# A causal convolution's last tiles: taps divided anew between four engines, and silus interleaved with products

## The chip, the cores and the metric

The kernel runs on one core of a Trainium2 chip. The metric is the device time of one execution in microseconds. Smaller is better. The engines are named as in the profile: PE is TensorE's matmul, PEld its weight load, DVE is VectorE, ACT is ScalarE, POOL is GpSimd and SP issues most DMAs.

## The reference

The program is a two-layer trunk of a streaming encoder, in float32, for 256 positions of 1024 channels. Each layer computes half a feed-forward block, a mixer, and half a feed-forward block, each on a normalized input and added to `h`. The mixer of the first layer is a convolution module, and the change is in it; that of the second is an attention.

```python
def conv_module(h, w_pw1, w_dw, g_norm, w_pw2):
    u = h @ w_pw1
    a, b = jnp.split(u, 2, axis=-1)
    u = a * jax.nn.sigmoid(b)
    u = lax.conv_general_dilated(          # causal, depthwise, width 31
        u, w_dw[:, None, :].astype(u.dtype), window_strides=(1,),
        padding=[(CONV_WIDTH - 1, 0)],
        dimension_numbers=("NWC", "WIO", "NWC"),
        feature_group_count=D_MODEL)
    u = jax.nn.silu(rmsnorm(u, g_norm))
    return u @ w_pw2
```

So each of 1024 channels is a sum over 31 taps, each a product of a shifted row with one weight per channel. The norm is over all channels of one position, so every channel has to be there before the first silu.

## The kernel before

**Layout.** Channels lie on the 128 partitions, in eight tiles (`k` from 0 to 7), and the 256 positions along the free axis, in two halves of 128, the first rows (`tb` = 0) and the second rows (`tb` = 1). `V` holds the gated input with 30 columns of zeros ahead of it, so that tap `j` of a tile is `V[:, k, j + start : j + stop]` times the column `dw[:, k, j]`.

**Who computes taps.** Three lists divide the 31 taps of each tile. An entry is (tile, first tap, end of taps, half), and half 2 means all 256 columns at once.

- `CONV_DVE`, in `taps_dve`: VectorE multiplies and accumulates in one instruction per tap, into two accumulators by turns (lines 777 and 779). Line 785 adds the two at the end.
- `CONV_POOL`, in `taps_pool`: per tap ScalarE makes a product (line 805, tile `prod`, six buffers) and GpSimd adds it (line 806), into two accumulators by turns. Line 816 adds the two. The first two taps are copies of ScalarE (line 801).
- `CONV_PE`, in `taps_pe`: TensorE multiplies with a diagonal matrix of the tap's weights (line 826). The diagonals are made long before, by ScalarE, beside the first feed-forward block. The taps of tiles 6 and 7 of one half share one PSUM bank `y`.

Tiles 6 and 7 (`CONV_LAST`) come last and are shared: in the first rows, tile 6 has 19 taps on ScalarE and GpSimd and 12 on TensorE, and tile 7 has 13 on VectorE and 18 on TensorE. In the second rows it is 19 and 12, and 24 and 7. The other tiles are each of one engine alone.

**The end of the convolution**, for each half, in `ends`:

1. Line 922: VectorE adds the parts of tile 6, then of tile 7 (`Y`).
2. Line 838: ScalarE squares each tile (`sq`). Line 844: TensorE adds the squares over the channels (`ms`), tile by tile in the order of `CONV_ORDER`; tiles 6 and 7 are last.
3. In `normed`: VectorE takes the mean (line 860, `msc`), GpSimd raises it to the power -1/2 (line 862, `rc`), ScalarE makes a diagonal of it (line 864, `dg`), TensorE spreads it over the partitions (line 866, `rb`).
4. For each tile: VectorE multiplies (line 871, `z`) and ScalarE takes the silu (line 873, `Z`). Tiles 4 to 7 come first (`rows_order`) and are used as they are. For tiles 0 to 3 the silu is also taken rounded (line 875, `Zh`), and VectorE makes the rest (line 876, `Zl`, "low").
5. The products with `cw2` into `o`: two plain matmuls for each of tiles 4 to 7 (line 954), then two times three split ones for each of tiles 0 to 3 (`mm3`, lines 280, 283 and 284). In the loop, `n` or `f` counts the tiles in the order of `rows_order`.

**What sets the order.** The framework's scheduler puts each engine's instructions in a fixed order, by dependencies, by priority (functions marked `urgent` go ahead), and by a timing of its own. `order(a, b)` is an edge that says only that `a` comes after `b`. The kernel uses it to place the totals and `rb` among TensorE's taps: `done[1]` is the list of TensorE's second-row taps, of which five stand ahead of the last total of the first rows, nine between it and `rb`, and five after `rb`. In `taps_dve`, `after` places four of VectorE's second-row taps ahead of the mean, five between the mean and the eight `z`, and the others behind. In `taps_pool`, the products of the second rows' tile 6 from the tenth tap on come after `dg`, and their adds after the power. In the products with `cw2`, the total of the second rows comes after the pair n = 4, `rb` after the pair n = 6, and the first column half of n = 7 after `rb`.

`load_ahead` starts the loads and casts of the next block's weights. A cast stands behind the latest urgent instructions of its engine.

Of the kernel before, what the change touches and what calls it, by code (L numbers as in the profile page):

```python
# [46 lines left out]

CONV_DVE = ((0, 0, 31, 0), (0, 0, 31, 1), (2, 0, 31, 2), (4, 0, 31, 2), (5, 0, 31, 2), (7, 0, 13, 0), (7, 0, 24, 1))  # L50
CONV_POOL = ((1, 0, 31, 0), (1, 0, 31, 1), (3, 0, 31, 2), (6, 0, 19, 0), (6, 0, 19, 1))
CONV_PE = ((6, 19, 31, 0), (7, 13, 31, 0), (6, 19, 31, 1), (7, 24, 31, 1))

CONV_MID = {3: 10, 5: 29}
CONV_FIRST = (0, 1)
CONV_LAST = (6, 7)

# [26 lines left out]
def trunk(ctx: ExitStack, tc: tile.TileContext, x, xt, pos, invf, gains, gfin, wdw,  # L84
# [21 lines left out]
    def bank(tag, name):  # L106
        return ps.tile([P, 512], F32, tag=tag, name=uid(name), bufs=BANKS[tag])
# [185 lines left out]
    def tbs(tb):  # L293
        return slice(tb * P, (tb + 1) * P)
# [423 lines left out]
    def conv_in(act, X, make_next):  # L718
# [46 lines left out]
        odd = {}  # L765
        slot = [0]

        def taps_dve(k, j0, j1, t, after={}):

            slot[0] ^= 1  # L770
            c = slice(slot[0] * S, slot[0] * S + t.stop - t.start)
            out = Y[:, k, t]
            for j in range(j0, j1):
                v, w = V[:, k, j + t.start:j + t.stop], dw[:, k, j:j + 1]
                y = acc[(j - j0) % 2][:, c]
                if j - j0 < 2:
                    ins = nc.vector.tensor_scalar(y, v, w, None, op0=ALU.mult)
                else:
                    ins = nc.vector.scalar_tensor_tensor(out if j == j1 - 1 else y, v, w, y, op0=ALU.mult, op1=ALU.add)  # L779
# [5 lines left out]
            nc.vector.tensor_add(out, acc[(j1 - j0) % 2][:, c], out)  # L785

        last_prod = [None]
        last_sum = [None]

        def taps_pool(k, j0, j1, t, after={}):  # L790

            if j1 - j0 < TAPS and k not in part:
                part[k] = act.tile([P, S], F32, name=uid("part"))
            if k not in odd:
                odd[k] = act.tile([P, S], F32, tag=f"odd{k % 2}", name=uid("odd"))
            y = [(part[k] if k in part else Y[:, k, :])[:, t], odd[k][:, t]]
            for j in range(j0, j1):
                v, w = V[:, k, j + t.start:j + t.stop], dw[:, k, j:j + 1]
                o = y[(j - j0) % 2]
                if j - j0 < 2:  # L800
                    nc.scalar.activation(o, v, AF.Copy, scale=w)
                else:
                    p = act.tile([P, S], F32, tag="prod", name=uid("prod"), bufs=6)
                    p = p[:, :t.stop - t.start]
                    prod = nc.scalar.activation(p, v, AF.Copy, scale=w)
                    ins = nc.gpsimd.tensor_tensor(o, o, p, op=ALU.add)
                    if last_prod[0] is not None:
                        order(prod, last_prod[0].ins)
                        order(ins, last_sum[0].ins)
                    if "power" in after and j >= j0 + 10:  # L810
                        order(prod, after["diagonal"].ins)
                        order(ins, after["power"].ins)
                    last_prod[0], last_sum[0] = prod, ins
                    if (k, j - j0, t.start) == (CONV_LAST[0], 7, 0):
                        nc_silu.append(prod)
            last_sum[0] = nc.gpsimd.tensor_tensor(y[0], y[0], y[1], op=ALU.add)
# [18 lines left out]
        def square(k, t):  # L835
            if k not in sq:
                sq[k] = act.tile([P, S], F32, tag="sq", name=uid("sq"), bufs=4)
            return nc.scalar.activation(sq[k][:, t], Y[:, k, t], AF.Square)
# [17 lines left out]
        @urgent  # L856
        def normed(tb, after=()):

            ms = small.tile([P, 1], F32, tag="msc", name=uid("msc"))
            mean = nc.vector.tensor_scalar(ms, msb[tb][:, :1], 1.0 / D, EPS, op0=ALU.mult, op1=ALU.add)  # L860
            rc = small.tile([P, 1], F32, tag="rc", name=uid("rc"))
            power = nc.gpsimd.tensor_tensor(rc, ms, neghalf, op=ALU.pow)
            dg = act.tile([P, P], F32, tag="dg", name=uid("dg"), bufs=2)
            diagonal = nc.scalar.activation(dg, ident, AF.Copy, scale=rc)
            rb = bank("AC"[tb], "rb")
            brow[tb] = nc.tensor.matmul(rb[:, :P], ones, dg, start=True, stop=True)
            for a in after:
                order(brow[tb], a.ins)
            for k in rows_order:
                z = act.tile([P, P], F32, tag="z", name=uid("z"), bufs=6)  # L870
                zi = nc.vector.tensor_mul(z, Y[:, k, tbs(tb)], rb[:, :P])
                g = G[:, g0 + k:g0 + k + 1]
                nc.scalar.activation(Z[:, k, tbs(tb)], z, AF.Silu, scale=g)
                if k < KT - CONV_PLAIN:
                    nc.scalar.activation(Zh[:, k, tbs(tb)], z, AF.Silu, scale=g)
                    nc.vector.tensor_sub(Zl[:, k, tbs(tb)], Z[:, k, tbs(tb)], Zh[:, k, tbs(tb)].bitcast(F32))
            return mean, power, diagonal, zi

        halves = (tbs(0), tbs(1), every)
        for items, f in ((CONV_DVE, taps_dve), (CONV_POOL, taps_pool)):  # L880
# [34 lines left out]
        def ends(tb, after, after_row):  # L915

            t = tbs(tb)

            @urgent
            def add():  # L920
                for k in CONV_LAST:
                    a = nc.vector.tensor_add(Y[:, k, t], y[tb][k], part[k][:, t] if k in part else Y[:, k, t])
# [8 lines left out]
            mean, power, diagonal, z = normed(tb, (after_row,))  # L931
            steps_of.update({0: a, 4: mean, 9: z, "power": power, "diagonal": diagonal})
# [12 lines left out]
        def mm(n, tb, d):  # L945
            f = rows_order[n]
            after = ()
            if (tb, d) == (0, 0):
                after = [brow[1]] if n == KT - 1 else ()
            w = loaded[conv_block[-1 - f // 2]]  # L950
            c = slice(f % 2 * D + d * 512, f % 2 * D + d * 512 + 512)
            start, stop = n == 0, n == KT - 1
            if f >= KT - CONV_PLAIN:
                return nc.tensor.matmul(o[tb, d], Z[:, f, tbs(tb)], w[:, c], start=start, stop=stop)  # L954
# [398 lines left out]
```

## Time and profile before

| what | value |
|---|---|
| median of 3 runs | 927.15 us (927.1 to 928.87) |
| the profiled execution | 927.98 us |
| its span, first to last instruction | 926.2 us |
| mean granted TensorE clock | 0.999 |
| TensorE busy | 912.5 us, 99% of the span |
| VectorE, ScalarE, GpSimd busy | 682.2, 537.2 and 224.9 us |
| taps on TensorE, tiles 6 and 7 | from 247.23 us on |
| first product with `cw2`, first rows | 261.27 us |
| first product with `cw2`, second rows | 275.04 us |

In the timeline a row gives start, length, engine, source line and operation, then the written tile, the read ones, the shapes and how many instructions are merged in the row. In brackets at its end stands how long the engine had been idle and which instruction ended that. The profile's span leaves out 1.78 us of the execution's time, which lie around it.

### The profile page before, as it was taken

What the parts mean: (1) busy time and instruction counts of PE and PEld (TensorE: products, weight loads), DVE (VectorE), ACT (ScalarE), POOL (GpSimd) and SP (SyncE); (2) the same over time, 40 slices, a digit from 0 to 9 for tenths busy, and PEclk for the clock granted to TensorE, in tenths of its full rate; (3) what the DMA queues carried; (4) which work ended last, traced back from release to release, by engine and by line L of the source; (5) the groups of instructions that cost most, each with busy time, mean ns of one, the idle gap of its engine ahead of it and who ended that gap; (6) DMA issues with size and microseconds to landing.
All of it is one profiled execution on the core that took longest, in us unless ns stands there. A gap on an engine that the chain in (4) does not pass through costs nothing.

```text
span 926.2 us, 12404 instructions
## 1 busy us (share of the span) xinstructions
PE 912.5 (99%) x4315; PEld 757.9 (82%) x4315; DVE 682.2 (74%) x1050; ACT 537.2 (58%) x932; POOL 224.9 (24%) x329
## 2 busy tenths in 40 slices
PE   8999999999999999999999999999999999999997
PEld 6888887898967888888888888888898778888886
DVE  5776877789967667787976667978666476667875
ACT  6955555669847545455574445555667374544653
POOL 0101232379921110232210003223200011003223
PEclk9999999999999999999999999999999999999999
DMA  9986556653306867566756675656441556774751
GB/s 331 346 278 232 186 191 213 251 182 138 138 1 245 297 231 233 182 193 225 281 219 235 228 245 176 200 213 246 182 183 46 182 206 243 251 246 135 227 192 46
DMA packets 60399, 191.58 MB, mean 207 GB/s; under 512 B 11184, under 2 KB 33328, under 8 KB 40752
## 3 DMA queue, kind: packets, MB, share of 16 engines
q1 hardware_dynamic: 59760, 190.09, 59.0%
q8 instruction: 34, 0.56, 0.2%
q10 hardware_dynamic: 576, 0.69, 0.2%
q14 instruction: 29, 0.24, 0.1%
HBM read 178.17 MB, written 12.58 MB: 206 GB/s over the span
## 4 chain that ended last, share of the span: by engine, by line
PE 85%; DVE 5%; ACT 3%; DMA 3%; issue 2%; POOL 1%; SPq 0%; POOLq 0%; ACTq 0%; DVEq 0%
PE u L284 16%; PE u L280 16%; PE u L283 16%; PE o L280 5%; PE o L283 5%; PE o L284 5%; DVE lo L171 3%; PE gate L734 3%; PE u L734 3%; DMA raw<-in_f1w 2%; PE o L954 2%; PE p L280 1%; PE p L283 1%; PE p L284 1%; ACT hi L167 1%
## 5 line engine op out<-in xcount | busy, mean ns | idle before, releaser
L171 DVE TENSOR_TENSOR lo<-raw,hi 128x1024 fp32r<-128x1024 f32 (+1 forms) x246 | 297.7, 1247 | 70.4 <-ACT hi L167 70.0
L167 ACT CAST hi<-raw 128x1024 fp32r<-128x1024 f32 (+1 forms) x250 | 248.0, 1046 | 143.7 <-PE u L284 108.4
L284 PE MATMUL u<-hi,Xl 128*128 128x512 f32 x688 | 267.8, 390 | 0.7 <-DVE Xl L341 0.7
L280 PE MATMUL u<-lo,Xh 128*128 128x512 f32 x688 | 268.1, 390 | 0.0
L283 PE MATMUL u<-hi,Xh 128*128 128x512 f32 x688 | 267.7, 389 | 0.0
L284 PEld LDWEIGHTS u<-hi,Xl 128*128 128x128 f32 x688 | 129.1, 188 | 28.4 <-DVE Xl L341 1.6
L280 PEld LDWEIGHTS u<-lo,Xh 128*128 128x128 f32 x688 | 129.1, 188 | 27.2 <-DVE lo L171 0.5
L283 PEld LDWEIGHTS u<-hi,Xh 128*128 128x128 f32 x688 | 129.1, 188 | 26.6
L181 POOL TENSOR_TENSOR sums<-raw 128x1024 f32<-128x1024 f32 x20 | 54.0, 2698 | 160.2 <-DMA raw<-in_f2w 51.4
L280 PE MATMUL o<-lo,Gh 128*128 128x512 f32 (+1 forms) x236 | 91.4, 387 | 0.7 <-DVE lo L171 0.7
L283 PE MATMUL o<-hi,Gh 128*128 128x512 f32 (+1 forms) x236 | 91.0, 386 | 0.0
L284 PE MATMUL o<-hi,Gl 128*128 128x512 f32 (+1 forms) x236 | 91.0, 386 | 0.0
L628 POOL TENSOR_TENSOR sx<-gb 128x128 f32<-128x128 f32 x20 | 10.4, 520 | 314.8 <-DMA gb<-gd 314.8
L620 ACT CAST Gh<-gb 128x512 fp32r<-128x512 f32 (+2 forms) x48 | 25.6, 539 | 68.0 <-DMA gb<-gd 67.8
L621 DVE TENSOR_TENSOR Gl<-gb,Gh 128x512 fp32r<-128x512 f32 (+2 forms) x48 | 33.2, 707 | 36.5 <-ACT Gh L620 36.5
L779 DVE SCALAR_TENSOR_TENSOR acc<-V,dw,acc 128x128 f32<-128x128 f32 (+1 forms) x171 | 57.5, 416 | 0.0
L189 ACT CAST hi<-sums 128x1024 fp32r<-128x1024 f32 x40 | 40.9, 1052 | 26.7 <-PE u L284 13.8
L190 DVE TENSOR_TENSOR lo<-sums,hi 128x1024 fp32r<-128x1024 f32 x40 | 56.1, 1435 | 0.0
L280 PEld LDWEIGHTS o<-lo,Gh 128*128 128x128 f32 x236 | 44.3, 188 | 10.8 <-DVE lo L171 2.0
L284 PEld LDWEIGHTS o<-hi,Gl 128*128 128x128 f32 x236 | 44.3, 188 | 9.0
L283 PEld LDWEIGHTS o<-hi,Gh 128*128 128x128 f32 x236 | 44.3, 188 | 8.8
L189 ACT CAST hi<-raw 128x512 fp32r<-128x512 f32 (+1 forms) x40 | 31.4, 833 | 28.2 <-PE o L284 23.3
(247 smaller groups left out, 1344.6 us busy)
## 6 DMA issues: line engine op xcount, KB each, us to landing
raw<-in_f2w SPq DMA_DIRECT2D x66, 1024.0 KB, 4.8
raw<-in_f1w SPq DMA_DIRECT2D x64, 1024.0 KB, 5.0
raw<-in_cw SPq DMA_DIRECT2D x12, 1024.0 KB, 5.1
gd<-gt SPq DMA_DIRECT2D x160, 64.0 KB, 2.7
gb<-gd SPq DMA_DIRECT2D x40, 256.0 KB, 2.9
raw<-in_wo SPq DMA_DIRECT2D x4, 1024.0 KB, 4.9
raw<-in_wuq SPq DMA_DIRECT2D x3, 1024.0 KB, 4.8
raw<-in_f1w SPq DMA_DIRECT2D x8, 256.0 KB, 6.5
```

Of the source, the lines that this page charges most:

```text
L167: behind(nc.scalar.copy(hi[:, c], raw[:, c]))
L171: behind(nc.vector.tensor_sub(lo[:, c], raw[:, c], hi[:, c].bitcast(F32)))
L181: behind(nc.gpsimd.tensor_tensor(t[:, 0:2, :], v[:, 0:4:3, :], v[:, 1:2, :].to_broadcast([P, 2, 512]), op=ALU.add))
L189: behind(nc.scalar.copy(hi[:, c0:c1], x[:, c0:c1]))
L190: behind(nc.vector.tensor_sub(lo[:, c0:c1], x[:, c0:c1], hi[:, c0:c1].bitcast(F32)))
L280: mm = nc.tensor.matmul(o, ah, bl, start=start, stop=False)
L283: nc.tensor.matmul(o, ah, bh, start=False, stop=False)
L284: return nc.tensor.matmul(o, al, bh, start=False, stop=stop)
L620: nc.scalar.copy(dh, x)
L621: nc.vector.tensor_sub(dl, x, dh.bitcast(F32))
L734: mm = nc.tensor.matmul(u[:, t], w[:, c], X.x[:, k, t], start=(k == 0), stop=(k == KT - 1))
L779: ins = nc.vector.scalar_tensor_tensor(out if j == j1 - 1 else y, v, w, y, op0=ALU.mult, op1=ALU.add)
```

## The change

The taps of tiles 6 and 7 are divided anew:

| | tile 6: ScalarE and GpSimd + TensorE | tile 7: VectorE + TensorE |
|---|---|---|
| first rows, before | 19 + 12 | 13 + 18 |
| first rows, after | 23 + 8 | 9 + 22 |
| second rows, before | 19 + 12 | 24 + 7 |
| second rows, after | 23 + 8 | 26 + 5 |

The other edits are edges of order. The sums of line 922 come after VectorE's last tap of the half. Of TensorE's 13 second-row taps, four stand ahead of the first rows' last total, five between it and `rb`, four after. The first rows' twelve silus stand in a fixed order, and the second rows' 13 later products are placed among them: two silus, five products, two silus, four products, two silus, two products, two silus, two products, four silus. The first rows' lows come after VectorE's last tap of the second rows. The second rows' last total comes ahead of the first column half of the pair n = 6, their `rb` may come from the pair n = 5 on, and `ends` and `load_ahead` are called one pair earlier.

```diff
-CONV_DVE = (..., (7, 0, 13, 0), (7, 0, 24, 1))
-CONV_POOL = (..., (6, 0, 19, 0), (6, 0, 19, 1))
-CONV_PE = ((6, 19, 31, 0), (7, 13, 31, 0), (6, 19, 31, 1), (7, 24, 31, 1))
+CONV_DVE = (..., (7, 0, 9, 0), (7, 0, 26, 1))
+CONV_POOL = (..., (6, 0, 23, 0), (6, 0, 23, 1))
+CONV_PE = ((6, 23, 31, 0), (7, 9, 31, 0), (6, 23, 31, 1), (7, 26, 31, 1))
+CONV_AMONG = ((1, 5), (3, 9), (5, 11), (7, 13))
...
-            nc.vector.tensor_add(out, acc[(j1 - j0) % 2][:, c], out)
+            last_tap[0] = nc.vector.tensor_add(out, acc[(j1 - j0) % 2][:, c], out)
...
                     if "power" in after and j >= j0 + 10:
-                        order(prod, after["diagonal"].ins)
                         order(ins, after["power"].ins)
+                        later.append(prod)
...
-                nc.scalar.activation(Z[:, k, tbs(tb)], z, AF.Silu, scale=g)
+                silus.append(nc.scalar.activation(Z[:, k, tbs(tb)], z, AF.Silu, scale=g))
                 if k < KT - CONV_PLAIN:
-                    nc.scalar.activation(Zh[:, k, tbs(tb)], z, AF.Silu, scale=g)
-                    nc.vector.tensor_sub(Zl[:, k, tbs(tb)], Z[:, k, tbs(tb)], Zh[:, k, tbs(tb)].bitcast(F32))
-            return mean, power, diagonal, zi
+                    silus.append(nc.scalar.activation(Zh[:, k, tbs(tb)], z, AF.Silu, scale=g))
+                    low = nc.vector.tensor_sub(Zl[:, k, tbs(tb)], Z[:, k, tbs(tb)], Zh[:, k, tbs(tb)].bitcast(F32))
+                    lows.append(low)
+            return mean, power, (silus, lows), zi
...
                     a = nc.vector.tensor_add(Y[:, k, t], y[tb][k], part[k][:, t] if k in part else Y[:, k, t])
+                    order(a, last_tap[0].ins)
                     square(k, t)
...
-        ends(0, done[1][4], done[1][13])
-        order(done[1][5], sums[0].ins)
-        order(done[1][14], brow[0].ins)
+        ends(0, done[1][3], done[1][8])
+        order(done[1][4], sums[0].ins)
+        order(done[1][9], brow[0].ins)
...
         taps(1)
+        silus, lows = steps_of["parts"]
+        order(lows[0], last_tap[0].ins)
+        for x, z in zip(silus, silus[1:]):
+            order(z, x.ins)
+        for i, prod in enumerate(later):
+            n = next(n for n, m in CONV_AMONG if i < m)
+            order(prod, silus[n].ins)
+            if (n, i + 1) in CONV_AMONG:
+                order(silus[n + 1], prod.ins)
...
-                after = [brow[1]] if n == KT - 1 else ()
+                after = [sums[1]] if n == KT - 2 else [brow[1]] if n == KT - 1 else ()
...
-                if tb == 0 and f == KT - 2:
+                if tb == 0 and f == KT - 3:
                     last_z = ends(1, first[1], now[1])
                     load_ahead()
```

More of the change, by code (lines that the diff above doesn't have):

```diff
@@ L46 @@
 FAST = (0, 2, 4, 6, 8)
-CONV_DVE = ((0, 0, 31, 0), (0, 0, 31, 1), (2, 0, 31, 2), (4, 0, 31, 2), (5, 0, 31, 2), (7, 0, 13, 0), (7, 0, 24, 1))
-CONV_POOL = ((1, 0, 31, 0), (1, 0, 31, 1), (3, 0, 31, 2), (6, 0, 19, 0), (6, 0, 19, 1))
-CONV_PE = ((6, 19, 31, 0), (7, 13, 31, 0), (6, 19, 31, 1), (7, 24, 31, 1))
+CONV_DVE = ((0, 0, 31, 0), (0, 0, 31, 1), (2, 0, 31, 2), (4, 0, 31, 2), (5, 0, 31, 2), (7, 0, 9, 0), (7, 0, 26, 1))
+CONV_POOL = ((1, 0, 31, 0), (1, 0, 31, 1), (3, 0, 31, 2), (6, 0, 23, 0), (6, 0, 23, 1))
+CONV_PE = ((6, 23, 31, 0), (7, 9, 31, 0), (6, 23, 31, 1), (7, 26, 31, 1))
 CONV_MID = {3: 10, 5: 29}
+CONV_AMONG = ((1, 5), (3, 9), (5, 11), (7, 13))
 CONV_FIRST = (0, 1)
@@ L766, in conv_in @@
         slot = [0]
+        last_tap = [None]
         def taps_dve(k, j0, j1, t, after={}):
@@ L784, in taps_dve @@
                 before = ins
-            nc.vector.tensor_add(out, acc[(j1 - j0) % 2][:, c], out)
+            last_tap[0] = nc.vector.tensor_add(out, acc[(j1 - j0) % 2][:, c], out)
         last_prod = [None]
         last_sum = [None]
+        later = []
         def taps_pool(k, j0, j1, t, after={}):
@@ L864, in normed @@
             diagonal = nc.scalar.activation(dg, ident, AF.Copy, scale=rc)
+            silus, lows = [], []
             rb = bank("AC"[tb], "rb")
@@ L930, in ends @@
             a = add()
-            mean, power, diagonal, z = normed(tb, (after_row,))
-            steps_of.update({0: a, 4: mean, 9: z, "power": power, "diagonal": diagonal})
-            return z
-        ends(0, done[1][4], done[1][13])
-        order(done[1][5], sums[0].ins)
-        order(done[1][14], brow[0].ins)
+            mean, power, parts, z = normed(tb, (after_row,))
+            steps_of.update({0: a, 4: mean, 9: z, "power": power, "parts": parts})
+            return z
+        ends(0, done[1][3], done[1][8])
+        order(done[1][4], sums[0].ins)
+        order(done[1][9], brow[0].ins)
         for x, mm in zip(done[1], done[1][1:]):
```

## The prediction

> **What bounds the kernel now.** I read the page first, for which engine fills the span, and the page's slices, for where it doesn't.
>
> ```profile
> PE 912.5 (99%) x4315; PEld 757.9 (82%) x4315; DVE 682.2 (74%) x1050; ACT 537.2 (58%) x932; POOL 224.9 (24%) x329
> PE   8999999999999999999999999999999999999997
> ```
>
> TensorE is busy for 912.5 us, and from the second slice to the last but one it shows 9 tenths. So TensorE sets the end: work taken off it, or a wait taken out of it, is worth its length, provided that nothing later waits for something that does not move along. The list of waits has no wait of TensorE between 288 and 420 us, the next feed-forward block. Therefore I read only the stretch that the change touches, 247 to 275 us, engine by engine in the timeline, in order of time. First TensorE (start, length, instruction, in brackets the idle time before it and who ended it):
>
> ```profile
> 250.13 4.93 PE L826 MATMUL y<-V,diag 128*128 128x128 f32 x42
> 254.90 0.50 PE L844 MATMUL ms<-ones,sq 128*128 128x1 f32 x4
> 255.27 0.91 PE L826 MATMUL y<-V,diag 128*128 128x128 f32 x6
> 256.02 0.28 PE L844 MATMUL ms<-ones,sq 128*128 128x1 f32 x2
> 256.89 0.38 PE L844 MATMUL ms<-ones,sq 128*128 128x1 f32 x2 [0.59 <-ACT sq L838]
> 257.14 2.25 PE L826 MATMUL y<-V,diag 128*128 128x128 f32 x18
> 259.23 0.39 PE L866 MATMUL rb<-dg,ones 128*128 128x128 f32 x2
> 259.45 1.28 PE L826 MATMUL y<-V,diag 128*128 128x128 f32 x10
> 261.27 7.13 PE L954 MATMUL o<-raw,Z 128*128 128x512 f32 x16 [0.54 <-ACT Z L873]
> ...
> 272.15 0.28 PE L844 MATMUL ms<-ones,sq 128*128 128x1 f32 x2
> ...
> 273.30 0.39 PE L284 MATMUL o<-hi,Zl 128*128 128x512 f32 x1
> 273.73 0.49 PE L866 MATMUL rb<-dg,ones 128*128 128x128 f32 x2
> ...
> 274.52 0.40 PE L284 MATMUL o<-hi,Zl 128*128 128x512 f32 x1
> 275.04 7.13 PE L954 MATMUL o<-raw,Z 128*128 128x512 f32 x16
> ```
>
> The source view of the line of the taps gives the count and the length of one:
>
> ```profile
> L826 PE MATMUL y<-V,diag x98: 274/275/356, 247.2 to 260.5; 128*128 128x128 f32 x98
> ```
>
> 98 records for 12 + 18 + 12 + 7 = 49 taps: two records each, so the 18 records at 257.14 are nine taps. They start (2.25 - 0.275)/17 = 0.116 us apart, and a tap costs 0.23 us. TensorE is held up at two named places in the first rows, 0.59 us before the last channel total and 0.54 us before the first product with `cw2`. In the second rows there are two small ones: matmuls of 512 columns leave 0.23 us apart, so after 273.30 the next could go at 273.53 and `rb` goes at 273.73 (0.20), and after 274.52 the next could go at 274.75 and goes at 275.04 (0.29). Together 1.62 us of waiting. This is all that a better order can win here; the rest must come from fewer taps.
>
> Who is late? VectorE for the 0.59 us:
>
> ```profile
> 251.71 0.60 DVE L777 TENSOR_SCALAR acc<-V,dw 128x128 f32<-128x128 f32 x2
> 252.22 2.15 DVE L779 SCALAR_TENSOR_TENSOR acc<-V,dw,acc 128x128 f32<-128x128 f32 x8
> 254.72 0.29 DVE L922 TENSOR_TENSOR Y<-y,part 128x128 f32<-128x128 f32 x1 [0.35 <-PE y L826]
> 254.93 0.61 DVE L779 SCALAR_TENSOR_TENSOR acc<-V,dw,acc 128x128 f32<-128x128 f32 x2
> 255.44 0.34 DVE L779 SCALAR_TENSOR_TENSOR Y<-V,dw,acc 128x128 f32<-128x128 f32 x1
> 255.82 0.29 DVE L785 TENSOR_TENSOR Y<-acc,Y 128x128 f32<-128x128 f32 x1
> 256.15 0.29 DVE L922 TENSOR_TENSOR Y<-y,Y 128x128 f32<-128x128 f32 x1
> ```
>
> Its 13 taps run to 256.11, with the sum of tile 6 in between, and only then comes the sum of tile 7 at 256.15. And ScalarE for the 0.54 us:
>
> ```profile
> 256.53 0.31 ACT L838 ACTIVATE sq<-Y 128x128 f32<-128x128 f32 x1 [1.17 <-DVE Y L922]
> 258.19 0.40 ACT L864 ACTIVATE dg<-ident,rc 128x128 f32<-128x128 f32 x1 [1.35 <-POOL rc L862]
> 258.50 2.43 ACT L805 ACTIVATE prod<-V,dw 128x128 f32<-128x128 f32 x8
> 260.83 0.68 ACT L873 ACTIVATE Z<-z,G 128x128 f32<-128x128 f32 x2
> ```
>
> The queue holds eight products between `dg` and the first silu; TensorE waits for that silu.
>
> **The change, part by part.** *TensorE's taps.* First rows: 8 + 22 = 30, as before. Second rows: 8 + 5 = 13 in place of 19. Six fewer at 0.23 us are 1.38 us less work on the bounding engine, if the waits don't grow.
>
> *VectorE's first rows.* Nine taps: two by 252.22, six at (2.15 - 0.34)/7 = 0.26 us to 253.77, the last and its closing sum 0.71 us (255.44 to 256.15), so free at 254.48. Both sums (L922) now come after that, but they also need TensorE's 30 taps: the 42 records from 250.13 hold 38 of the first rows, and 250.13 + 37 x 0.116 + 0.275 = 254.70, which is when the sum at 254.72 was let go. So the sums stand at 254.72 and 254.93 instead of 254.72 and 256.15. What is queued behind the new wait on VectorE is the second rows' taps, which gain over a microsecond. The square comes 0.38 us after the sum (256.15 to 256.53), at 255.31, and its total can start 0.36 us later (256.53 to 256.89), at 255.67.
>
> *TensorE up to the totals.* From 250.13 + 38 x 0.116 = 254.54 it has four second-row taps (0.93), the total of tile 5 (254.90 to 255.27, 0.37) and that of tile 6 (256.89 to 257.14, 0.25): the last total goes at 256.09, against 256.89. The 0.59 us wait is gone, and what is late next is TensorE itself.
>
> *From the last total to the first product.* The second rows show this chain with nothing in its way: total to `rb` 1.58 us (272.15 to 273.73), `rb` to product 1.31 (273.73 to 275.04). In the first rows VectorE has a tap in hand when the mean is asked for, at most half a tap (0.17) more: `rb` at 257.84. TensorE, with the total (0.25) and five taps (1.15) behind 256.09, is there at 257.49 and waits 0.35. After `rb` (0.22) it has four taps (0.92) and is done at 258.98; the silu permits 259.15. This requires that the first two silus stand ahead of the products, which the new edges force.
>
> *GpSimd.* Tile 6 has four more adds in each half:
>
> ```profile
> 252.00 0.46 POOL L816 TENSOR_TENSOR part<-part,odd 128x128 f32<-128x128 f32 x1
> 252.41 0.46 POOL L806 TENSOR_TENSOR part<-part,prod 128x128 f32<-128x128 f32 x1
> ...
> 255.30 0.45 POOL L806 TENSOR_TENSOR odd<-odd,prod 128x128 f32<-128x128 f32 x1
> 257.61 0.55 POOL L862 TENSOR_TENSOR rc<-msc,neghalf 128x1 f32<-128x1 f32 x1 [1.85 <-DVE msc L860]
> ```
>
> Eight adds lie from 252.41 to 255.30, 0.413 us apart. Four more make the first rows' closing sum start at 253.65 and end at 254.11, still 0.6 us ahead of the sum that reads it (254.72): nothing, and if that cover went, each further add would cost 0.41. But the eight adds of the second rows now run to about 257.36, while the power wants GpSimd at 257.61 less 0.80 = 256.81. Behind the seventh, which ends at 256.95, it waits 0.14; behind all eight it waits 0.55. I take 0.14, since the seventh's end is the first moment at which it can be picked: first product at 259.3, gain 261.27 - 259.3 = 1.97 us (bounds 2.12 and 1.57).
>
> *Second rows.* From the first product TensorE needs 7.13 us for four plain tiles, then 24 split matmuls. The last total must now precede the pair n = 6, `rb` only n = 7. The chain from total to next product is 272.15 to 275.04 = 2.89 us; behind the total now stand 12 matmuls at 0.23 and `rb` (0.22), 2.98 us, where eight stood. That covers 0.49 us of waiting up to 0.1; I take 0.4 (bounds 0 and 0.49). It needs the total ready when TensorE gets there, at 259.3 + 7.13 + 6 x 0.23 = 267.8 at the earliest:
>
> ```profile
> 263.30 0.29 DVE L876 TENSOR_TENSOR Zl<-Z,Zh 128x128 fp32r<-128x128 f32 x1
> ```
>
> VectorE: eight `z` from about 258.5 to 260.2, 17 taps at 0.26, closing step 0.71: 265.3. ScalarE: 12 silus and 13 products from 258.8 at 0.29 us (the two silus at 260.83 take 0.68, one 0.39): the thirteenth product at about 264.9. GpSimd's last add follows to 265.5, its closing sum to 265.9; then sum (0.29), square (0.38) and total (0.36): 266.9. So the new order of silus and products hides behind 7.13 us of products, with 0.9 us to spare. `load_ahead` is called one pair earlier in the program; its casts stay tied behind the second rows' silus and its DMAs keep their place in the queue: nothing.
>
> *Sum.* 1.97 + 0.4 = 2.4 us against the profiled execution's own 927.98: 925.6. The three runs have their median at 927.15, 0.83 below it, so the forecast for the median is 924.8.
>
> **The rivals.**
>
> *Squares and products swap on ScalarE.* If the scheduler puts the first rows' two squares ahead of the second rows' eight early products, these start at 255.6, their adds at about 256.1, the eighth ends at 259.4 (256.1 + 8 x 0.413), and a power behind them starts then instead of at 256.81: first product at 261.75, 0.5 us later than now; the second rows' 0.4 gives most of it back. Time about 928.1, no change, with every mix between this and the forecast. For it: in the new timing a square is ready at 255.05 and the eighth product gets its buffer at about 254.9, nearly a tie. Against it: before, all eight went ahead.
>
> *Slower: the hand-overs between ScalarE and GpSimd.* The products now come in four batches between silus. GpSimd's only such wait so far is the one that ends with a product:
>
> ```profile
> 259.02 0.46 POOL L806 TENSOR_TENSOR part<-part,prod 128x128 f32<-128x128 f32 x1 [0.87 <-ACT prod L805]
> ```
>
> If every batch cost GpSimd such a gap and more, tile 6's sum, and with it the total that TensorE must pass before n = 6, is late, and everything behind it in TensorE's queue stands still. The spare is 0.9 us, plus up to 1.4 if the total is queued behind the pair n = 5; from there lateness costs its length. The forecast is eaten up at 0.9 + 2.4 = 3.3 us, and 0.2% (1.85 us, about what a measurement of this kernel can tell from no change) is lost at 5.2 us, four gaps of 1.3. With four gaps of 1.4 the time is 927.98 - 2.4 + 5.6 - 0.9 = 930.3. Against it: ScalarE makes a product in 0.29 us, GpSimd uses one in 0.41, so a batch of five leaves a store that covers two silus.
>
> *Lows beside the last adds.* The low parts (L876, 0.29 each) now come after VectorE's last tap, around 265.3, where GpSimd still adds. If one holds up the other, tile 6's sum is late by up to four lows, 1.16 us, 0.3 over the spare: 925.9. The Trainium skill, SBUF — State Buffer, Who interferes with whom, states that a VectorE instruction with both inputs in SBUF, as these are, excludes a GpSimd instruction that reads SBUF. No row here shows it: the low at 263.30 found GpSimd finished.
>
> **How the numbers follow.** Forecast 0.46 (own range 924.2 to 925.3, from 3.0 us, six taps and every wait, down to the power behind all eight adds and some of the 0.4 lost); lows 0.10, still over 0.2% faster; swap and its mixes 0.28, within 0.2%; slower 0.16, which holds the hand-overs and whatever else a changed order of queues holds up. Faster 0.56, same 0.28, slower 0.16. The range goes from 923.9 (the low end less a quarter of a microsecond, for the scatter of runs) to 928.0 (the swap's 927.3 and part of what lies above): 923.9 to 928.0.
>
> **What would show it.** In the changed profile: 13 second-row taps; no wait before the last total of the first rows, which stands at about 256.1; two silus directly behind `dg`; the first product at 259.0 to 259.7; the second rows' first product 13.3 to 13.8 us after it; and all later work earlier by the same amount. I am wrong if the power starts after 258, if a TensorE wait on `sq` or `Zl` appears between 266 and 271 us, or if the gain at 275 us is lost again later.

## The result, and the profile after

| | kernel before | kernel after |
|---|---|---|
| median | 926.14 us (22 runs, 925.06 to 928.87) | 924.40 us (22 runs, 923.27 to 926.72) |
| profiled execution / its span | 927.98 / 926.2 us | 926.72 / 924.8 us |
| granted TensorE clock | 0.999 | 0.998 |

The ratio after to before is 0.9980, with a 95% interval from 0.9973 to 0.9987: faster by 0.2%, 1.2 to 2.5 us. The forecast was 924.8 us and a gain of 2.4 us. The absolute number is closer than the working deserves, and that is luck: in the longer series the kernel before has its median 1.0 us lower than in the three runs that the forecast started from, and the gain is about 0.6 us smaller than forecast.

The page of the kernel after, engines:

```profile
PE 911.3 (99%) x4303; PEld 756.8 (82%) x4303; DVE 681.9 (74%) x1048; ACT 539.5 (58%) x940; POOL 226.9 (25%) x337
```

TensorE has 12 instructions and 1.2 us less. The source view of the line of the taps, after, has 86 records, 43 taps, where it had 98 records:

```profile
L831 PE MATMUL y<-V,diag x86: 274/275/356, 246.9 to 258.8; 128*128 128x128 f32 x86
```

With 30 in the first rows, 13 are left for the second. Now the timeline of TensorE, after (start, length, instruction, in brackets the idle time before it and who ended it):

```profile
255.47 0.51 PE L849 MATMUL ms<-ones,sq 128*128 128x1 f32 x4
255.84 1.36 PE L831 MATMUL y<-V,diag 128*128 128x128 f32 x10
257.69 0.49 PE L872 MATMUL rb<-dg,ones 128*128 128x128 f32 x2 [0.49 <-ACT dg L869]
258.02 1.06 PE L831 MATMUL y<-V,diag 128*128 128x128 f32 x8
259.00 7.13 PE L972 MATMUL o<-raw,Z 128*128 128x512 f32 x16
...
270.01 0.47 PE L286 MATMUL o<-hi,Zl 128*128 128x512 f32 x1
270.32 0.28 PE L849 MATMUL ms<-ones,sq 128*128 128x1 f32 x2
270.46 0.47 PE L282 MATMUL o<-lo,Zh 128*128 128x512 f32 x1
270.78 0.40 PE L285 MATMUL o<-hi,Zh 128*128 128x512 f32 x1
271.01 0.40 PE L286 MATMUL o<-hi,Zl 128*128 128x512 f32 x1
271.92 0.49 PE L872 MATMUL rb<-dg,ones 128*128 128x128 f32 x2 [0.51 <-ACT dg L869]
272.16 0.48 PE L282 MATMUL o<-lo,Zh 128*128 128x512 f32 x1
272.48 0.40 PE L285 MATMUL o<-hi,Zh 128*128 128x512 f32 x1
272.71 0.40 PE L286 MATMUL o<-hi,Zl 128*128 128x512 f32 x1
273.22 7.13 PE L972 MATMUL o<-raw,Z 128*128 128x512 f32 x16
```

In the first rows no wait stands before the totals, 0.49 us stand before `rb` and none before the first product. In the second rows only three split matmuls stand between the last total (270.32) and `rb`, and three more between `rb` and the next product: six behind the total, where eight stood before and twelve were forecast.

TensorE has the same 1168 records in the same order up to the first tap of tiles 6 and 7, yet that tap starts at 247.23 us before, at 246.91 after, and anywhere from 244.53 to 247.77 in the runs below: this start scatters by more than the change is worth. So I measure the stretch in the trace from its own beginning: from TensorE's first tap of tiles 6 and 7 to the first product of the second rows, split at the first product of the first rows.

| stretch, us | before | after | change |
|---|---|---|---|
| first tap to first product, first rows | 14.05 | 12.09 | -1.96 |
| from there to the first product, second rows | 13.76 | 14.22 | +0.46 |
| together | 27.81 | 26.31 | -1.50 |

The spans differ by 1.4 us: 0.32 from the earlier start, 1.50 from the stretch, and 0.44 given back behind it (644.21 us from the stretch's end to the last matmul before, 644.65 after). Of this I put only the stretch down to the change. Behind the stretch most of the kernels below take 644.1 to 644.2 us, as before, e5 takes 644.5, and e7 and e9 take more (see there). Of the 0.44 us here, 0.42 are lost in one place: at 443.55 us TensorE waits for the low part of a weight (`lo`, line 173). VectorE makes that part behind a sum that waits for GpSimd, and GpSimd waits for a load: its instruction starts 164.3 us behind the stretch, where it starts 161.6 to 163.7 us behind it in the kernel before and in e1 to e5, none of which has this wait. Whether the change makes the load late is not shown.

### The profile page after: what moved, and what is told of

It reads as the page before. It is cut to its first block, busy times and chain, and to the rows that moved or that the text cites. A ratio compares the mean times of both kernels' runs of the same rounds, so it can differ in the third digit from the quotient of the medians.

```text
span 924.8 us, 12403 instructions
## 1 busy us (share of the span) xinstructions
PE 911.3 (99%) x4303; PEld 756.8 (82%) x4303; DVE 681.9 (74%) x1048; ACT 539.5 (58%) x940; POOL 226.9 (25%) x337
## 4 chain that ended last, share of the span: by engine, by line
PE 77%; DVE 7%; DMA 5%; ACT 5%; issue 3%; POOL 2%; SPq 1%; POOLq 0%; DVEq 0%; ACTq 0%
PE u L286 16%; PE u L282 16%; PE u L285 16%; PE o L282 4%; PE o L285 4%; PE o L286 4%; DVE lo L173 4%; PE gate L736 3%; PE u L736 3%; DMA raw<-in_f1w 2%; POOL sums L183 2%; PE o L972 2%; ACT hi L169 1%; DVE lo L192 1%; DMA raw<-in_f2w 1%
## 5 line engine op out<-in xcount | busy, mean ns | idle before, releaser
L191 ACT CAST hi<-sums 128x1024 fp32r<-128x1024 f32 x40 | 41.0, 1052 | 30.7 <-PE u L286 14.2
L810 ACT ACTIVATE prod<-V,dw 128x128 f32<-128x128 f32 (+1 forms) x129 | 48.4, 418 | 3.4 <-POOL Y L811 1.4
```

The lines of the kernel that those rows point to most:

```text
L191: behind(nc.scalar.copy(hi[:, c0:c1], x[:, c0:c1]))
```

## The experiments

What had to be told apart: why the second rows lost 0.46 us. My theory after reading the trace: the new edge in the products with `cw2` stands only at the first column half (`d` = 0), six matmuls of n = 6 and 7. The 12 split matmuls of the second half are bound by nothing, the scheduler put them ahead of the totals, and so the cover behind the total is missing. The rival: the total's inputs are late, whatever the edges say. The second question was how the first rows' 1.96 us divide between the taps and the edges. All times are from the stretch as defined above; "first" is first tap to first product of the first rows, "second" is from there to the first product of the second rows.

| kernel | first | second | together | split matmuls behind the last total | median, us | ratio to before, 95% |
|---|---|---|---|---|---|---|
| before | 14.05 | 13.76 | 27.81 | 8 | | |
| after | 12.09 | 14.22 | 26.31 | 6 | 924.40 | 0.9973 to 0.9987 |
| e1_both_halves | 12.10 | 13.44 | 25.55 | 12 | 923.68 | 0.9963 to 0.9986 |
| e2_total_first | 12.09 | 13.18 | 25.27 | 18 | 922.90 | 0.9955 to 0.9979 |
| e5_old_second | 12.12 | 14.91 | 27.03 | 3 | 925.09 | 0.9978 to 0.9995 |
| e3_taps_only | 13.14 | 14.22 | 27.36 | 6 | 925.50 | 0.9983 to 1.0000 |
| e4_edges_only | 12.77 | 13.66 | 26.43 | 8 | 924.99 | 0.9977 to 0.9995 |
| e8_three_ahead | 12.11 | 13.18 | 25.29 | 18 | 923.88 | 0.9962 to 0.9984 |
| e7_24 | 12.11 | 13.16 | 25.27 | 18 | 925.84 | 0.9982 to 1.0000 |
| e9_24_three | 12.09 | 13.17 | 25.25 | 18 | 925.01 | 0.9980 to 0.9998 |
| e10_power_soon | 11.69 | 13.18 | 24.86 | 18 | 922.75 | 0.9957 to 0.9979 |
| e11_power_sooner | 11.69 | 13.18 | 24.86 | 18 | 922.50 | 0.9956 to 0.9980 |

The column of split matmuls is the key to the second one: the more of the 24 stand behind the last total, the shorter the second rows, in the order 3, 6, 8, 12, 18. The kernel before, run beside them, had medians of 926.36 (e1 to e4), 926.37 (e5 to e9) and 925.71 us (e10, e11). Each stretch is read from one profiled execution. Where kernels have the same edges and taps in a part, these readings agree within 0.03 us: 12.09 to 12.12 us for the first rows of the kernel after, e1, e2 and e5, and 13.18 us for the second rows of e2, e8, e10 and e11. The whole times tell less: their intervals are 1.3 to 2.2 us wide, and those of e3 and e7 reach 1.0000, so the whole time doesn't show these two to be faster than before. What follows therefore rests on the stretch.

**e1_both_halves: the edges at both column halves.**

```diff
-            if (tb, d) == (0, 0):
-                after = [sums[1]] if n == KT - 2 else [brow[1]] if n == KT - 1 else ()
+            if tb == 0:
+                after = [sums[1]] if n == KT - 2 else [brow[1] if d == 0 else sums[1]] if n == KT - 1 else ()
```

> The changed kernel, but in the second rows' end both column halves of n = 6, and the second half of n = 7, come after the second rows' last total (the change puts only the first column half there). Theory (the scheduler moved the total behind the six matmuls of the second column half that carried no edge, so only three matmuls stand between the total and rb): nine matmuls now stand between total and rb, three behind rb; no wait at rb, 0.4 us at the product; second product 13.5 us after the first, against 14.22 in the changed kernel and 13.77 in the one before; 0.7 us faster than the changed kernel. Rival (the total is late because its inputs are: 23 adds, 26 taps, lows): TensorE waits for sq at the total, and the second product stays 14.2 us after the first.

Measured: second rows 13.44 us. The timeline of TensorE, e1:

```profile
266.36 0.50 PE L849 MATMUL ms<-ones,sq 128*128 128x1 f32 x4
...
268.88 0.38 PE L872 MATMUL rb<-dg,ones 128*128 128x128 f32 x2
...
269.57 0.40 PE L286 MATMUL o<-hi,Zl 128*128 128x512 f32 x1
270.08 4.13 PE L972 MATMUL o<-raw,Z 128*128 128x512 f32 x9
```

Both totals go together, without a wait, and `rb` follows nine matmuls later without one. The next matmul could go 0.23 us after 269.57 and goes 0.51 after: 0.28 us of the chain are left uncovered behind `rb`. The inputs of the totals were there in time, so the rival is out.

**e2_total_first: the total one pair earlier still, `rb` between n = 6 and n = 7.**

```diff
-            if (tb, d) == (0, 0):
-                after = [sums[1]] if n == KT - 2 else [brow[1]] if n == KT - 1 else ()
+            if tb == 0:
+                after = [sums[1]] if n in (KT - 3, KT - 2) else [brow[1]] if n == KT - 1 else ()
...
-                if tb == 0 and f == KT - 3:
+                if tb == 0 and f == KT - 4:
...
+                if tb == 0 and f == KT - 2:
+                    order(brow[1], now[0].ins)
+                    order(brow[1], now[1].ins)
```

> The changed kernel, but the second rows' last total stands right behind the pair n = 4, twelve matmuls between it and rb, and both halves of n = 7 behind rb. Theory: twelve matmuls (2.75 us) cover total to rb (1.58), six (1.37) cover rb to product (1.31); no wait is left in the second rows; second product 13.3 us after the first, 0.9 us faster than the changed kernel. Rival (inputs late): a wait for sq of up to 0.9 us at the total, since it stands 1.4 us earlier than in the other variant, and no gain.

Measured: 13.18 us. The timeline of TensorE, e2:

```profile
265.14 0.50 PE L849 MATMUL ms<-ones,sq 128*128 128x1 f32 x4
...
268.34 0.38 PE L872 MATMUL rb<-dg,ones 128*128 128x128 f32 x2
...
269.73 0.39 PE L286 MATMUL o<-hi,Zl 128*128 128x512 f32 x1
269.96 4.45 PE L972 MATMUL o<-raw,Z 128*128 128x512 f32 x10
```

The product follows the last split matmul by 0.23 us: nothing is uncovered any more. The totals of tiles 6 and 7 go together from 8.36 us after the first product (256.78) on, and even there they don't wait, while in the kernel after the last one went at 11.33. Against the kernel after, 1.04 us come from placing these two instructions.

**e5_old_second: the rest of the change with the second rows' edges of before.**

```diff
-                after = [sums[1]] if n == KT - 2 else [brow[1]] if n == KT - 1 else ()
+                after = [brow[1]] if n == KT - 1 else ()
...
-                if tb == 0 and f == KT - 3:
+                if tb == 0 and f == KT - 2:
```

> The changed kernel with the second rows' end as before (total behind the pair n = 4, rb behind the pair n = 6, no edge from the total to n = 6). Theory (where no edge binds, the scheduler puts the total late in TensorE's queue once the taps are divided anew; the change's own edge is of some use): the scheduler now puts the total behind 21 of the 24 split matmuls and rb directly after it; a wait of 1.4 us at rb; second product 14.9 us after the first, 0.7 us slower than the changed kernel. Rival (the change's edges of the second rows cause the loss): second product 13.8 us after the first, as before the change.

Measured: 14.91 us. The timeline of TensorE, e5:

```profile
268.71 0.28 PE L849 MATMUL ms<-ones,sq 128*128 128x1 f32 x2
270.30 0.49 PE L872 MATMUL rb<-dg,ones 128*128 128x128 f32 x2 [1.31 <-ACT dg L869]
```

With the old edges the scheduler puts the last total behind 21 of the 24 split matmuls, `rb` stands directly behind it, and TensorE waits 1.31 us. So the change's own edge was not useless: it saved 0.69 us against this. What had made the total's place worse was the rest of the change: the same old edges of the second rows leave eight split matmuls behind the total in the kernel before, six with the new division alone (e3) and three here.

**e3_taps_only: the kernel before with the new division of the taps, and nothing else but the counts that belong to it.**

```diff
-... (7, 0, 13, 0), (7, 0, 24, 1))
-... (6, 0, 19, 0), (6, 0, 19, 1))
-CONV_PE = ((6, 19, 31, 0), (7, 13, 31, 0), (6, 19, 31, 1), (7, 24, 31, 1))
+... (7, 0, 9, 0), (7, 0, 26, 1))
+... (6, 0, 23, 0), (6, 0, 23, 1))
+CONV_PE = ((6, 23, 31, 0), (7, 9, 31, 0), (6, 23, 31, 1), (7, 26, 31, 1))
...
-        ends(0, done[1][4], done[1][13])
-        order(done[1][5], sums[0].ins)
-        order(done[1][14], brow[0].ins)
+        ends(0, done[1][3], done[1][8])
+        order(done[1][4], sums[0].ins)
+        order(done[1][9], brow[0].ins)
```

> The kernel before with the new division of the taps and TensorE's taps placed around total and rb as in the change, and with no other edge of the change: products after dg, no order among silus and products, the second rows' total and rb as before. Theory: the 0.59 us wait goes and the total comes about 0.85 us earlier as in the change, but the first silu stands behind eight or more products: first product about 13.4 us after TensorE's first tap (before 14.04, changed 12.09), a wait of 1.2 us or more for Z; second product 13.8 us after the first; 0.6 us faster than before. Rival (the division alone is the gain): first product 12.1 to 12.4 us after the first tap.

Measured: first rows 13.14 us, second 14.22. Timelines of ScalarE and of TensorE, e3:

```profile
256.19 2.14 ACT L805 ACTIVATE prod<-V,dw 128x128 f32<-128x128 f32 x7
258.23 0.68 ACT L873 ACTIVATE Z<-z,G 128x128 f32<-128x128 f32 x2
```

```profile
258.67 7.13 PE L954 MATMUL o<-raw,Z 128*128 128x512 f32 x16 [0.95 <-ACT Z L873]
```

`rb` goes as early as after the whole change (10.80 us behind the first tap, 10.79 there), but the silu stands behind seven products and TensorE waits 0.95 us for it. So the difference to the whole change, 13.14 - 12.09 = 1.05 us, lies behind `rb`, where TensorE waits for the silu: it is what the two silus ahead of the products are worth once `rb` is this early. No kernel here has these two silus ahead without the other edges. The second rows have the 14.22 us of the kernel after although none of the change's edges of the second rows is in this kernel: the new division of the taps alone brings the scheduler to place the total late.

**e4_edges_only: the kernel after with the old division of the taps.**

```diff
-... (7, 0, 9, 0), (7, 0, 26, 1))
-... (6, 0, 23, 0), (6, 0, 23, 1))
-CONV_PE = ((6, 23, 31, 0), (7, 9, 31, 0), (6, 23, 31, 1), (7, 26, 31, 1))
+... (7, 0, 13, 0), (7, 0, 24, 1))
+... (6, 0, 19, 0), (6, 0, 19, 1))
+CONV_PE = ((6, 19, 31, 0), (7, 13, 31, 0), (6, 19, 31, 1), (7, 24, 31, 1))
...
-CONV_AMONG = ((1, 5), (3, 9), (5, 11), (7, 13))
+CONV_AMONG = ((1, 5), (3, 9))
...
-        ends(0, done[1][3], done[1][8])
-        order(done[1][4], sums[0].ins)
-        order(done[1][9], brow[0].ins)
+        ends(0, done[1][4], done[1][13])
+        order(done[1][5], sums[0].ins)
+        order(done[1][14], brow[0].ins)
```

> The changed kernel's edges with the old division of the taps (two silus, five products, two silus, four products, then the other silus). Theory: the 0.59 us wait before the total stays, the silu is ready when TensorE has done its nineteen taps: first product about 13.4 us after TensorE's first tap (before 14.04, changed 12.09); second rows lose as in the change, 14.2 us; about as fast as before. Rival (the order of silus alone is the gain): first product 12.5 us or less after the first tap.

Measured: first rows 12.77 us, better than I expected, and second rows 13.66, not 14.2. Timelines of VectorE and of TensorE, e4:

```profile
254.61 0.29 DVE L789 TENSOR_TENSOR Y<-acc,Y 128x128 f32<-128x128 f32 x1
254.81 0.28 DVE L929 TENSOR_TENSOR Y<-y,part 128x128 f32<-128x128 f32 x1
```

```profile
258.08 0.39 PE L872 MATMUL rb<-dg,ones 128*128 128x128 f32 x2
259.43 7.03 PE L972 MATMUL o<-raw,Z 128*128 128x512 f32 x16
```

In the kernel before, the sum of tile 6 stood among VectorE's taps and made it wait 0.35 us for TensorE. With the edge "sums behind the last tap" that wait is gone, even with 13 taps: the second record of the last total starts 9.23 us after the first tap instead of 9.80. No wait is left before `rb` or before the first product either, so in e4 TensorE's own 49 taps set the first rows, but for some 0.1 us at the totals, whose row is 0.64 us long instead of 0.50. Edges alone -1.28 us, taps alone -0.91, both -1.96, less than the two together: six taps fewer are 1.38 us less work, but with the edges in place they bring only 12.77 - 12.09 = 0.68, because TensorE then waits for `rb`. And in the second rows 14.22 - 13.66 = 0.56 us are lost by the place of the total, which e1 and e2 mend. So over the whole stretch the edges alone win 1.38 us, and the new division of the taps adds only 0.12 (26.43 to 26.31).

**e8_three_ahead, e7_24 and e9_24_three: is the total held by TensorE's queue?** All three start from e2. In e8 only three second-row taps, not four, stand ahead of the last total of the first rows; in e7 GpSimd takes one more tap of tile 6 in each half, TensorE one less; e9 is both.

```diff
# e8, and e9
-        ends(0, done[1][3], done[1][8])
-        order(done[1][4], sums[0].ins)
+        ends(0, done[1][2], done[1][8])
+        order(done[1][3], sums[0].ins)
# e7, and e9
-... (6, 0, 23, 0), (6, 0, 23, 1))
-CONV_PE = ((6, 23, 31, 0), (7, 9, 31, 0), (6, 23, 31, 1), (7, 26, 31, 1))
+... (6, 0, 24, 0), (6, 0, 24, 1))
+CONV_PE = ((6, 24, 31, 0), (7, 9, 31, 0), (6, 24, 31, 1), (7, 26, 31, 1))
-CONV_MID = {3: 10, 5: 29}
+CONV_MID = {3: 10, 5: 28}
-CONV_AMONG = ((1, 5), (3, 9), (5, 11), (7, 13))
+CONV_AMONG = ((1, 5), (3, 9), (5, 12), (7, 14))
```

> The variant with the second rows' total behind n = 4, and three instead of four of TensorE's second-row taps ahead of the first rows' last total, six between it and rb. Theory: the square is there 0.2 us before TensorE; the total goes 0.17 us earlier, and so does rb, whose wait falls from 0.5 to 0.1 us; first product 11.9 us after the first tap. Rival (the chain, not TensorE's place, sets the total): total at the same time, a wait for sq of 0.2 us, first product at 12.1.

> The variant with the second rows' total behind n = 4, and one more tap of tile 6 moved from TensorE to ScalarE and GpSimd in both halves (24 + 7). Theory (the first rows' chain starts with the sum that waits for TensorE's thirty taps): 29 taps let the sum go 0.2 us earlier; first product 11.9 us after the first tap instead of 12.09, second 13.2 us after it; 0.2 us faster than that variant. Rival: GpSimd's 24th tap now ends last, or the power waits for it: no gain or up to 0.2 us slower.

> Both: tile 6 divided 24 + 7 and three taps ahead of the first rows' last total, with the second rows' total behind n = 4. Theory: first product 11.7 us after the first tap, second 13.2 us after the first; 0.35 us faster than the variant with the second rows' total behind n = 4 alone, about 3 us faster than the kernel before. Rival: the two gains are one (11.9).

Measured: first rows 12.11, 12.11 and 12.09 us, unmoved. In e8 the total waits for the square instead, so the row of the totals is 0.72 us long where it is 0.51 after, and the second record of the last one starts at the same 8.81 us. The timelines of TensorE, e8, and of GpSimd, e7:

```profile
254.26 0.72 PE L849 MATMUL ms<-ones,sq 128*128 128x1 f32 x4
```

```profile
254.16 0.47 POOL L811 TENSOR_TENSOR odd<-odd,prod 128x128 f32<-128x128 f32 x1
254.57 0.56 POOL L867 TENSOR_TENSOR rc<-msc,neghalf 128x1 f32<-128x1 f32 x1
```

In e7 the total does go 0.15 us earlier (8.67 instead of 8.82), and the power starts behind GpSimd's add at 254.57, 9.76 us after the first tap, as in the kernel after (256.65 - 246.91 = 9.74). The earlier total is lost in GpSimd's queue. Moreover e7 and e9 lose outside the stretch: from the next feed-forward block's first matmul to the end they take 634.4 and 632.9 us, where the others and the kernel before take 630.8 to 631.3. The list of waits of e7 between 860 and 925 us has a line that e2 and the kernel after lack:

```profile
PE o L282 <- DVE lo L173: 1.7, 3, 0.8
```

Weights come late in the last feed-forward block, which is about half of what e7 loses. Why they are late, and what the other half is, stays open.

**e10_power_soon and e11_power_sooner: fewer adds ahead of the power.** Both start from e2 and let fewer of the second rows' early adds go ahead of the power: six (e10) and four (e11) instead of seven, the products staying where they are.

```diff
-                    if "power" in after and j >= j0 + 10:
+                    if "power" in after and j >= j0 + 8:      # e11: j0 + 6
                         order(ins, after["power"].ins)
+                    if "power" in after and j >= j0 + 10:
                         later.append(prod)
```

> The variant with the second rows' total behind n = 4, and two more of GpSimd's second-row adds placed behind the first rows' power: six stand ahead of it in GpSimd's queue, where the scheduler had put seven. Theory (in the changed kernel the power waits 0.4 us for the seventh add, and this sets the first rows' chain): the power starts 0.4 us earlier, rb's wait for dg falls from 0.5 to 0.1 us, first product 11.7 us after the first tap instead of 12.09; 0.4 us faster than that variant. Rival (the mean, on VectorE, or TensorE's taps set the chain): first product at 12.1.

> The same with four adds ahead of the power. Theory: with GpSimd idle the power starts when the mean is there, as with six adds; no further gain, first product 11.7 us after the first tap; GpSimd's last sum of the second rows may come 0.4 us later, hidden behind TensorE. Rival (each add ahead costs its 0.41 us): first product 10.9.

Measured: 11.69 us in both. Timelines of GpSimd in the kernel after, in e10 and in e11:

```profile
256.24 0.47 POOL L811 TENSOR_TENSOR part<-part,prod 128x128 f32<-128x128 f32 x1
256.65 0.56 POOL L867 TENSOR_TENSOR rc<-msc,neghalf 128x1 f32<-128x1 f32 x1
```

```profile
253.87 0.46 POOL L811 TENSOR_TENSOR odd<-odd,prod 128x128 f32<-128x128 f32 x1
254.34 0.55 POOL L868 TENSOR_TENSOR rc<-msc,neghalf 128x1 f32<-128x1 f32 x1
```

```profile
257.11 0.55 POOL L868 TENSOR_TENSOR rc<-msc,neghalf 128x1 f32<-128x1 f32 x1 [0.81 <-DVE msc L866]
```

The power starts 254.34 - 244.99 = 9.35 us after the first tap instead of 9.74, the timeline lists no wait before `rb` any more, and the product comes 0.40 us earlier. With four adds GpSimd stands idle 0.81 us and nothing more is won: now the power starts when the mean is there. In the stretch both kernels win more than the change does, 2.95 us against 1.50. The measured gain, 0.32% of 925.71 us, is 3.0 us (2.0 to 4.0), which overlaps with the 1.2 to 2.5 us of the change.

## Why the prediction was right, and where it was wrong

*Six taps fewer:* right, 43 taps, and 1.2 us less on TensorE's page against 1.38.

*First rows, 1.97 us:* right, 1.96. Measured from the first tap, the power was forecast at 256.95 - 247.23 = 9.72 us and stands at 9.74; the product was forecast at 12.07 and is at 12.09. That the wait before `rb` reads 0.49 us, as the 0.35 and 0.14 of the forecast add up to, is a coincidence of two ways of counting: the forecast counts from the moment at which the next matmul could leave, and so counted (255.84 + 10 x 0.116 = 257.00 to 257.69) the wait is 0.69. Two sizes were off without effect. TensorE was there 0.17 us earlier than I reckoned, at 257.00 - 246.91 = 10.09 us instead of 257.49 - 247.23 = 10.26. The other is the mean. The timeline of VectorE, after:

```profile
254.41 0.29 DVE L929 TENSOR_TENSOR Y<-y,part 128x128 f32<-128x128 f32 x1 [0.29 <-PE y L831]
254.61 0.28 DVE L929 TENSOR_TENSOR Y<-y,Y 128x128 f32<-128x128 f32 x1
...
256.02 0.16 DVE L865 TENSOR_SCALAR msc<-ms 128x1 f32<-128x1 f32 x1
```

The sums stand 7.50 us after the first tap, as forecast. The mean is ready earlier than I allowed for: in e10, where no add is in the way, the power starts at 9.35 instead of the 9.58 (256.81 - 247.23) that I gave as the moment at which it is wanted. So it waited some 0.39 us for GpSimd, not 0.14. The power was bound by GpSimd's seventh add either way, which is why the sum held, and behind that add lay a further 0.4 us that e10 then took.

*Second rows, 0.4 us gained:* wrong, 0.46 lost. The step that failed is "behind the total now stand 12 matmuls at 0.23 and `rb`". I read the edge as if it bound a pair of tile matmuls in both column halves; the code binds `(tb, d) == (0, 0)` alone. The rest of that step was sound: the chain took 2.90 us (270.32 to 273.22, forecast 2.89), and with twelve matmuls behind the total, in e1, the second rows take 13.44 us, 0.32 less than before. The total's inputs were in time, as argued; but nothing told the scheduler to put the total ahead of the whole pair. Of my signs, the second rows' first product was to come 13.3 to 13.8 us after the first; it came 14.22 after, and this sign showed the step to be wrong. The wait on `sq` or `Zl` between 266 and 271 us did not come: the waits stand at `rb` (0.51) and before the product (0.28), later and for the chain itself. The last sign, that the gain is lost again later, came in part: the 0.44 us behind the stretch.

*What the edges on ScalarE do:* right in kind. The timeline of ScalarE, after, has two silus directly behind `dg`, then the products in batches:

```profile
254.26 0.40 ACT L810 ACTIVATE prod<-V,dw 128x128 f32<-128x128 f32 x1 [0.55 <-POOL part L811]
254.73 0.31 ACT L843 ACTIVATE sq<-Y 128x128 f32<-128x128 f32 x1
254.95 0.39 ACT L810 ACTIVATE prod<-V,dw 128x128 f32<-128x128 f32 x1
255.24 0.29 ACT L843 ACTIVATE sq<-Y 128x128 f32<-128x128 f32 x1
257.24 0.40 ACT L869 ACTIVATE dg<-ident,rc 128x128 f32<-128x128 f32 x1 [1.71 <-POOL rc L867]
258.54 0.69 ACT L879 ACTIVATE Z<-z,G 128x128 f32<-128x128 f32 x2 [0.90 <-DVE z L877]
```

The same rows answer the first rival: squares and products did swap in part, one product between two squares. Tile 7's square at 255.24 came 0.35 us after its sum had ended (254.61 + 0.28 = 254.89), where tile 6's came after 0.03. That cost nothing: TensorE has no wait before the totals, and the power had to wait 0.39 us for GpSimd in any case.

*The hand-overs:* no cost. The timeline of GpSimd, after:

```profile
259.67 0.46 POOL L811 TENSOR_TENSOR part<-part,prod 128x128 f32<-128x128 f32 x1 [2.04 <-ACT prod L810]
...
264.64 0.61 POOL L811 TENSOR_TENSOR odd<-odd,prod 128x128 f32<-128x128 f32 x1 [0.30 <-ACT prod L810]
265.20 0.46 POOL L811 TENSOR_TENSOR part<-part,prod 128x128 f32<-128x128 f32 x1
265.74 0.45 POOL L821 TENSOR_TENSOR part<-part,odd 128x128 f32<-128x128 f32 x1
```

GpSimd waits 2.04 us at the first batch, as it must, and then 0.30 once, not four times 1.4. Its last sum ends at 266.19, 7.2 us after the first product where I had 6.6 (265.9 - 259.3): later, but ahead of any need, as e2 shows with its total at 8.36.

*Lows beside the last adds:* the rival's mechanism is there, its price is not. And I was wrong that no row of the kernel before shows it: the rows of another block do (both below).

## What to carry to other kernels

An edge in front of some of an engine's independent instructions binds only those: the scheduler may put all the others ahead, so count, in the code, how many instructions are really forced behind the early one, and look at its place in the queue first. When a short instruction of a critical chain runs on an engine with queued background work, as the power behind GpSimd's adds here, read the moment at which it is wanted and the moment at which it starts; the difference (0.39 us) was invisible in the waits, because the engine was busy. And when two kernels share a long program whose start scatters by microseconds, compare them over the stretch that differs, from an event just before it.

## What the runs showed of the hardware

Lows and adds do hold each other up. The timeline of VectorE, after:

```profile
264.65 0.28 DVE L882 TENSOR_TENSOR Zl<-Z,Zh 128x128 fp32r<-128x128 f32 x1
265.40 0.40 DVE L882 TENSOR_TENSOR Zl<-Z,Zh 128x128 fp32r<-128x128 f32 x1 [0.48 <-ACT Zh L881]
```

The add that starts with the low at 264.65 takes 0.61 us where the others take 0.45 to 0.47, and the low that starts at 265.40, in the middle of the add at 265.20, takes 0.40 where its neighbours take 0.28 or 0.29; e2 and e10 have the same pair of numbers within 0.01. So it costs 0.11 to 0.15 us for each meeting here, less than the 0.29 for each low that the rival charged, and it is hidden: the sums that follow are done by 266.71 (266.43 + 0.28), and the total goes at 270.32. The Trainium skill, SBUF — State Buffer, Who interferes with whom, states that such a VectorE instruction, with both inputs in SBUF, contends with a GpSimd instruction that reads SBUF; the trace agrees.

The kernel before shows it at larger prices, in a feed-forward block. The source view of line 628, before, where GpSimd subtracts 128x128 tiles:

```profile
L628 POOL TENSOR_TENSOR sx<-gb,gb x20: 458/468/1442, 45.9 to 864.8; 128x128 f32<-128x128 f32 x20
```

The one of 1.44 us starts at 107.25, inside a subtraction of VectorE (`lo` from `raw` and `hi`, line 171) that runs from 106.89 to 108.37, and it ends 0.32 us after that one. The 33 instructions of that line that take over 0.6 us all end 0.32 or 0.33 us after a VectorE instruction with two inputs in SBUF, and so does the add of 0.61 us above, 0.32 us after its low (264.93 to 265.25). So GpSimd gets on only when VectorE's instruction is over, and the price is small in this stretch because a low is short.

VectorE's taps, whose accumulator is in PSUM, lengthen no add: beside them the adds take 0.45 to 0.47 us, which agrees with that section too: by it, a VectorE instruction with at most one input in SBUF does not contend.
